# Row norms of half the tiles from a natural-layout load, split query halves kept apart, and new times in the order planner of a two-layer attention trunk

## The chip, the cores and the metric

One core of one Trainium2 chip runs the whole program. The metric is device time in microseconds of one execution; each time given as a result is the median of several executions.

## The reference

A trunk of two layers works on x of 1024 rows by 1024 columns, float32. Each layer adds to x the product of an output matrix with a gated attention result: `x <- x + W_out(mixer(RMSNorm(x)) * silu(gate))`, where one input projection gives queries, keys, values and the gate.

- RMSNorm divides each row of x by the root of its mean square, so it needs one sum of squares for each of the 1024 rows.
- Layer A: 16 query heads of 64 and 2 key heads; each query sees itself and the 127 keys before it, with a learned sink in the softmax.
- Layer B: three groups of 16 query heads and 4 key heads, with (window, dilation) = (128, 1), (512, 4), (2048, 16). The three results are merged for each position by their softmax denominators.
- Queries and keys are normalised for each head, and their first 16 of 64 dimensions are rotated by position.

## The kernel before

**Tiling.** The 1024 rows are 8 row tiles of 128 (`t` or `u`). Columns of the model are 8 blocks of 128 (`k`). Every float32 product is made from two parts: a value is split into a high part in a reduced format (ScalarE, a copy) and a low part, the rest (VectorE or GpSimd, a subtraction), and TensorE makes three products, high by high, high by low, low by high (`split`, line 438; `mm3`, line 500). For each of four sets of heads `n`, `load_w` (452) loads and splits the weights (`raw` to `wt`), and `proj_tile` (505) makes 24 matmuls into `psz` for a row tile, which ScalarE copies to `z`, in layer A with the row's factor `ra`. `z` goes to DRAM (`za`, `zb`) and comes back as `zi` in the order of rows that its group of heads needs (`fetch`, 716).

**Attention of one tile.** `prep` (548) has GpSimd square and rotate, VectorE sum the squares, GpSimd raise to a power (`r`), and TensorE transpose queries and keys into `pq`. ScalarE and VectorE then write the split queries `qs`. Its two halves `two` are the two heads of a pair: ScalarE writes the high part of a half into the upper 64 partitions, VectorE reads that and writes the low part into the lower 64 (lines 571 to 577). `attend` (594) makes the scores `pss`, VectorE adds the mask and takes the minimum (`pe`, with sums of the tile into `nm` or `st`), ScalarE takes the exponential, TensorE transposes it (`ptt`), ScalarE and VectorE split it (`pp`), and TensorE multiplies by the values (`po`). `merge` (642) scales the results: the factors `cr` go to DRAM (`cd`) and come back spread over partitions as `cb`, and VectorE multiplies each result by its `cb`.

**The first row norms.** In the first set of layer A (lines 819 to 846), x arrives transposed by the host (`xt`, partitions are columns). For each row tile it is loaded (`load_xt`, 394) and split into `hT`; then GpSimd squares the whole tile into `sqx`, VectorE sums over `k` into `sr` (rows of the tile along the free side), TensorE transposes `sr` into `pr` in PSUM, VectorE sums that into `ss` (tile `nss`), and `rstd` (470) has GpSimd turn it into `ra`, which scales `z`. `pr` uses a ring of one PSUM buffer that other transposes share (`NB["pM"]` is 1). `sqx` uses a ring of two buffers with the tag `p`, of which the scores `pe` are later users. Later norms (`norm_scale`, 477) take x in natural layout and let ScalarE square and sum in one instruction.

**The order of work.** No loop order is kept. Every call is recorded with its tile regions (`Plan.add`, 172), which are compared element by element for overlaps. `Plan.forward` (209) then plays the program with a priced duration for each instruction (`_price`, 299): each engine takes the ready instruction with the best priority. `backward` (251) makes new priorities from the end, and `issue` (283) tries this for some rounds and keeps the order with the shortest played time. That order is written out for each of the engines, and each engine runs its list strictly in order; all DMAs stand in the one list of SP. A price has two parts, the time until the engine is free and the time until the result is there. A DMA is priced with the issue time `ISSUE`, a fixed time and its bytes at 300 GB/s. All engines' instructions are recorded by a helper, so that the profile puts them on one line (352).

Of the kernel before, what the change touches and what calls it, by code (L numbers as in the profile page):

```python
# [12 lines left out]
F32 = mybir.dt.float32  # L13
F32R = mybir.dt.float32r
# [4 lines left out]
P = 128  # L19
# [27 lines left out]
SECB = 0  # L47
KL = 4
SA = 2
TRIP = 1900  # L50
ROUNDS = 8
SB = 4
YA = 4
# [44 lines left out]
class Plan:  # L98
# [9 lines left out]
           ("POOL", "PE"): 100, ("POOL", "ACT"): 32, ("POOL", "DVE"): 33, ("POOL", "POOL"): 83, ("POOL", "SP"): 100}  # L108
    LOAD = 94
    DRAIN = 25  # L110
    ISSUE = 475

    def __init__(self, tc):
        self.tc, self.nc = tc, tc.nc
# [94 lines left out]
    def forward(self, prio, users):  # L209
        ops, n = self.ops, len(self.ops)  # L210
        left = [len(o[2]) for o in ops]
        start, ready_at = [0.0] * n, [0.0] * n
        free = {e: 0.0 for e in self.ENGINES}
        done = {e: 0.0 for e in self.ENGINES}
        moved = {e: False for e in self.ENGINES}
        future = {e: [] for e in self.ENGINES}
        ready = {e: [] for e in self.ENGINES}
        dma, loaded, order = 0.0, None, []
        for i in range(n):
            if not left[i]:  # L220
                heapq.heappush(future[ops[i][0]], (0.0, i))
        while len(order) < n:
            s, e = min((free[e] if ready[e] else max(free[e], future[e][0][0]), k, e)
                       for k, e in enumerate(self.ENGINES) if ready[e] or future[e])[::2]
            while future[e] and future[e][0][0] <= s:
                i = heapq.heappop(future[e])[1]
                heapq.heappush(ready[e], (prio[i], i))
            i = heapq.heappop(ready[e])[1]
            _, _, _, occ, _, func, dur, _, moves = ops[i]
            wait = 0.0  # L230
            if e == "SP":
                free[e] = s + self.ISSUE
                wait = max(0.0, dma - s - 1100)
                dma = max(dma, s + 1100) + occ
            else:
                if func not in (None, loaded):
                    loaded = func
                    s += 1283
                if moves or moved[e]:
                    s = max(s, done[e] + self.DRAIN)  # L240
                free[e], done[e], moved[e] = s + occ, s + dur, moves
            start[i] = s
            order.append(i)
            for j, t in users[i]:
                ready_at[j] = max(ready_at[j], s + t + wait)
                left[j] -= 1
                if not left[j]:
                    heapq.heappush(future[ops[j][0]], (ready_at[j], j))
        return order, start, max(s + ops[i][6] for i, s in enumerate(start))
# [49 lines left out]
def _price(eng, name, out, ins, kw):  # L299

    n = out.free_size()
    if eng == "SP":
        t = out.size() * 4 / 300.0
        return t, t + 1100 + TRIP
    if eng == "PE":
        t = max(108, (P if name == "transpose" else n) / 2.4 + 13)
        return t, t + 165
    steps = [abs(st) for st, k in out.ap[1:] if k > 1]
    held = any(a.free_size() == 1 for a in ins[1:]) and n > 1
    accum = kw.get("accum_out") is not None  # L310
    if eng == "ACT":
        t = 70 + 0.84 * n + (70 if held else 0) + (0 if ins[0].space == bass.MemoryType.PSUM else 65)
        return (t + 93, t + 73) if accum else (t, t + 90)
    if eng == "DVE":
        if name == "tensor_reduce":
            last = ins[0].ap[-1][0]
            t = 75 + (1.04 if last == 1 else 1.78) * ins[0].free_size()
        elif name == "reciprocal":
            t = 100 + 8 * n
        elif name == "tensor_scalar":  # L320
            t = 130 + 0.53 * n
        else:
            wide = 2.1 if steps and min(steps) >= 4 and n >= 2 * P else 1.04
            t = 70 + wide * n
            t += 80 if name in ("tensor_tensor_reduce", "scalar_tensor_tensor") else 0
        return t, t + 75
    if kw.get("op") is OP.pow:
        t = 270 + 172 * n
    elif n <= 8:
        t = 300  # L330
    else:
        t = 1.95 * n if n > 512 else (50 if 200 < n < 400 else 160) + 2.1 * n
    return t, t + 55
# [23 lines left out]
def trunk(ctx, tc, x, norm_a, w_in_a, q_gain_a, k_gain_a, sinks_a, w_out_a,  # L357
# [190 lines left out]
    def prep(kind, order, tpos, z, nh, kv, slot):  # L548
        w = nh * HD
        sq = nc.tile(sp, [P, 320], F32, tag="sq", bufs=1, name="sq")  # L550
        nc.gpsimd.tensor_tensor(sq[:, :w], z[:, :w], z[:, :w], op=OP.mult)
        ss = nc.tile(sp, [P, 5], F32, tag="ss", bufs=2, name="ss")
        nc.vector.tensor_reduce(ss[:, :nh], sq[:, :w].rearrange("p (h d) -> p h d", d=HD), axis=AX, op=OP.add)
        r = nc.tile(sp, [P, 5], F32, tag="r", bufs=3, name="r")
        rstd(r[:, :nh], ss[:, :nh], 1.0, HD * EPS)
        zr = z[:, :w].rearrange("p (h d) -> p h d", d=HD)[:, :, :ROT]
        t0 = nc.tile(sp, [P, 5, ROT], F32, tag="t0", bufs=1, name="t0")[:, :nh]
        t1 = nc.tile(sp, [P, 5, ROT], F32, tag="t1", bufs=1, name="t1")[:, :nh]
        nc.gpsimd.tensor_tensor(t0, zr, rg[:, kind, :nh], op=OP.mult)
        c_, s_ = cs[:, order, tpos, 0], cs[:, order, tpos, 1]  # L560
        nc.gpsimd.tensor_tensor(t1, t0, c_[:, None, :].to_broadcast([P, nh, ROT]), op=OP.mult)
        hf = ROT // 2
        nc.gpsimd.tensor_tensor(zr[:, :, :hf], t0[:, :, hf:],
                                s_[:, None, :hf].to_broadcast([P, nh, hf]), op=OP.mult)
        nc.gpsimd.tensor_tensor(zr[:, :, hf:], t0[:, :, :hf],
                                s_[:, None, hf:].to_broadcast([P, nh, hf]), op=OP.mult)
        nc.gpsimd.tensor_tensor(zr, zr, t1, op=OP.add)
        pm = nc.tile(pM, [P, 4, P], F32, tag="m", bufs=NB["pM"], name="pq")
        for pr in range(2):
            nc.tensor.transpose(pm[:, pr], z[:, pr * P:(pr + 1) * P], ident)  # L570
        qs = nc.tile(sp, [P, 2, 2, P], F32R, tag="qs", bufs=2, name="qs")
        gq = gc[:, 0, kind:kind + 1]
        for two in range(2):
            rows = slice(two * HD, two * HD + HD)
            nc.scalar.activation(qs[:HD, :, two], pm[rows, 0:2], AF.Copy, scale=gq[rows])
            nc.vector.scalar_tensor_tensor(qs[HD:, :, two], pm[rows, 0:2], gq[rows], f(qs[:HD, :, two]),
                                           op0=OP.mult, op1=OP.subtract)
        if kv is not None:
            kd, vt = kv
            kh, kl = kd[:, 0], kd[:, 1]  # L580
            kk = nc.tile(sp, [P, 2, HD], F32, tag="kk", bufs=2, name="kk")
            nc.gpsimd.tensor_scalar(kk, z[:, None, 4 * HD:5 * HD].to_broadcast([P, 2, HD]), r[:, 4:5], -8.0,
                                    op0=OP.mult, op1=OP.mult)
            nc.tensor.transpose(pm[:, 2], kk.rearrange("p a b -> p (a b)"), ident)
            gk = gc[:, 1, kind:kind + 1]
            nc.scalar.activation(kh[:, slot], pm[:, 2], AF.Copy, scale=gk)
            nc.vector.scalar_tensor_tensor(kl[:, slot], pm[:, 2], gk, f(kh[:, slot]),
                                           op0=OP.mult, op1=OP.subtract)
            zv = z[:, 5 * HD:6 * HD]
            nc.scalar.activation(vt[:, slot, :HD], zv, AF.Copy)  # L590
            nc.gpsimd.tensor_tensor(vt[:, slot, HD:], zv, f(vt[:, slot, :HD]), op=OP.subtract)
        return qs, r
# [220 lines left out]
    for n in range(4):  # L813
# [5 lines left out]
        if n == 0:  # L819
            zd = tc.dram_tile([T, width], F32, name="za0")  # L820
            for t in range(NT):
# [2 lines left out]
                for k in range(0, NK, 4):  # L824
                    split(*(a[:, k:k + 4, t % 2 * P:(t % 2 + 1) * P] for a in hT[t // 2]), xr[:, k:k + 4])
                nc.bias = 0
                sq = nc.tile(sp, [P, NK, P], F32, tag="p", bufs=2, name="sqx")
                if t < SQ:
                    nc.scalar.activation(sq, xr, AF.Square)
                else:  # L830
                    nc.gpsimd.tensor_tensor(sq, xr, xr, op=OP.mult)
                sr = nc.tile(sp, [P, P], F32, tag="zi", bufs=3, name="sr")
                nc.vector.tensor_reduce(sr, sq.rearrange("p k t -> p t k"), axis=AX, op=OP.add)
                pr = nc.tile(pM, [P, 4, P], F32, tag="m", bufs=NB["pM"], name="pr")
                nc.tensor.transpose(pr[:, 0], sr, ident)
                ss = nc.tile(sp, [P, 1], F32, tag="nss", bufs=2, name="nss")
                nc.vector.tensor_reduce(ss, pr[:, 0], axis=AX, op=OP.add)
                rstd(ra[:, t:t + 1], ss, 1.0 / D, EPS)
                if t == LC:
                    late_constants()  # L840
# [222 lines left out]
```

## Time and profile before

| | us |
|---|---|
| median of 3 runs | 1289.6 |
| lowest, highest | 1288.63, 1290.04 |
| the profiled execution | 1286.87 |
| its span, first to last instruction | 1285.0 |
| mean granted TensorE clock | 0.999 |
| ScalarE, VectorE, GpSimd busy | 880.5, 1028.3, 708.3 |
| moved by DMAs | 149.74 MB, 117 GB/s over the span |

The profile is of one execution. PE is TensorE's matmuls, PEld its weight loads, which overlap them, DVE is VectorE, ACT ScalarE, POOL GpSimd, SP the queue that issues the DMAs. Idle time of an engine is put down to what ended it. A wait of an engine that is not the bottleneck costs nothing by itself.

### The profile page before, as it was taken

The page shows a single profiled execution, that of the slowest core. Times are in us where ns is not written, and L with a number is a line of the kernel's source. Part 1 is how long each engine was busy: PE and PEld are TensorE (multiplying, and loading weights), DVE is VectorE, ACT ScalarE, POOL GpSimd, SP SyncE. Part 2 cuts the span into 40 slices and gives each one's busy share as a digit, 9 for nine tenths or more (in the row PEclk, how much of TensorE's full clock was granted, in tenths as well). Part 3 has the DMA queues.
Part 4 walks back from the last instruction along what each step waited for, and adds up shares of the span by engine and source line. Part 5 has one row for each costly group of instructions (what it writes and reads, how often), then busy time and mean ns, then how long its engine had stood idle before and what let it go on. Part 6 is the DMA issues. An engine that isn't in the chain of part 4 may idle for free. (4 is left out here: it accounts for less than half of the span.)

```text
span 1285.0 us, 25754 instructions
## 1 busy us (share of the span) xinstructions
PE 1244.5 (97%) x7851; PEld 1136.3 (88%) x7851; DVE 1028.3 (80%) x2968; ACT 880.5 (69%) x2377; POOL 708.3 (55%) x1388
## 2 busy tenths in 40 slices
PE   7999999999999999999999999999999999999998
PEld 6999899998688999989888999988999988998776
DVE  8668888777955428878888878889888989779896
ACT  5367686877733437877767887767887766987661
POOL 5655455455500038556567655477656567786632
PEclk9999999999999999999999999999999999999999
DMA  6423223245444233223233323244233244454525
GB/s 226 141 76 103 84 80 117 81 146 178 123 129 140 99 104 99 81 71 111 93 125 122 91 73 111 88 139 135 79 95 91 94 130 128 140 174 129 173 80 181
DMA packets 142666, 149.74 MB, mean 117 GB/s; under 512 B 33576, under 2 KB 129344, under 8 KB 142528
## 3 DMA queue, kind: packets, MB, share of 16 engines
q1 hardware_dynamic: 142528, 148.09, 36.7%
q8 instruction: 63, 1.03, 0.3%
q14 instruction: 75, 0.61, 0.2%
HBM read 105.57 MB, written 42.47 MB: 115 GB/s over the span
## 5 line engine op out<-in xcount | busy, mean ns | idle before, releaser
L352 PE MATMUL psz<-wt,hT 128*128 128x384 f32 (+1 forms) x3072 | 632.9, 343 | 5.7 <-DVE wt L352 2.8
L352 PEld LDWEIGHTS psz<-wt,hT 128*128 128x128 f32 x3072 | 510.8, 190 | 16.2 <-DVE wt L352 3.6
L352 PE MATMUL psg<-hT,wt 128*128 128x256 f32 x1536 | 220.3, 291 | 0.3 <-DVE gT L352 0.3
L352 PEld LDWEIGHTS psg<-hT,wt 128*128 128x128 f32 x1536 | 200.3, 191 | 2.3 <-PE psg L352 0.5
L352 ACT ACTIVATE pe<-pe,st 128x128 f32<-128x128 f32 (+1 forms) x384 | 169.1, 442 | 36.2 <-DVE st L352 33.7
L352 PE MATMUL ptt<-ident,pe 128*128 128x128 f32 x800 | 170.8, 275 | 2.8 <-ACT pe L352 2.6
L352 DVE SCALAR_TENSOR_TENSOR qs<-pq,gt,qs 64x256 fp32r<-64x256 f32 x256 | 123.9, 484 | 44.8 <-ACT qs L352 38.5
L352 DVE TENSOR_TENSOR pp<-ptt,pp 128x512 fp32r<-128x512 f32 x200 | 131.5, 684 | 32.2 <-ACT pp L352 30.6
L352 POOL TENSOR_TENSOR r<-r,ex 128x5 f32<-128x5 f32 (+1 forms) x128 | 150.6, 1176 | 5.6
L352 ACT ACTIVATE qs<-pq,gt 64x256 fp32r<-64x256 f32 x256 | 120.1, 469 | 42.9 <-PE pq L352 36.2
L352 DVE SCALAR_TENSOR_TENSOR wt<-raw,gt,wt 128x384 fp32r<-128x384 f32 (+1 forms) x188 | 114.5, 639 | 28.5 <-ACT wt L352 26.6
L352 ACT ACTIVATE pp<-ptt 128x512 fp32r<-128x512 f32 x200 | 111.9, 595 | 35.9 <-PE ptt L352 35.1
L352 ACT ACTIVATE oh<-po 64x512 f32<-64x512 f32 x128 | 76.0, 594 | 82.2 <-PE po L352 78.5
L352 DVE CUSTOM_DVE_ANT_0 pe<-pss,con,r 128x256 f32<-128x256 f32 x288 | 123.5, 477 | 8.9 <-PE pss L352 8.5
L352 PEld LDWEIGHTS ptt<-ident,pe 128*128 128x128 f32 x800 | 105.7, 140 | 21.8 <-ACT pe L352 9.8
L352 ACT ACTIVATE wt<-raw,gt 128x384 fp32r<-128x384 f32 (+1 forms) x188 | 98.9, 564 | 19.6 <-DMA raw<-in_w_in_b_dram 6.9
L352 PE MATMUL po<-pp,vring 128*128 128x512 f32 x280 | 106.9, 416 | 3.8 <-ACT pp L352 1.5
L352 POOL TENSOR_SCALAR r<-ss 128x5 f32<-128x5 f32 (+1 forms) x128 | 30.3, 237 | 144.7 <-DVE st L352 55.5
L352 PE MATMUL psw<-hT,wy 128*128 128x512 f32 x384 | 107.8, 408 | 2.0 <-ACT wy L352 1.2
L352 POOL TENSOR_TENSOR sq<-zi 128x320 f32<-128x320 f32 (+1 forms) x128 | 93.8, 733 | 25.3 <-DMA zi<-za 9.8
L352 PE MATMUL pss<-kring,qs 128*128 128x256 f32 x560 | 99.3, 286 | 2.5 <-DVE kring L352 2.3
L352 POOL TENSOR_TENSOR t<-zi,rg 128x80 f32<-128x80 f32 (+1 forms) x128 | 48.4, 378 | 93.3 <-DMA zi<-zb 60.2
(142 smaller groups left out, 2175.3 us busy)
## 6 DMA issues: line engine op xcount, KB each, us to landing
raw<-in_w_in_b_dram SPq DMA_DIRECT2D x96, 192.0 KB
zb<-z SPq DMA_DIRECT2D x96, 192.0 KB
cb<-cd SPq DMA_DIRECT2D x128, 128.0 KB
zi<-zb SPq DMA_DIRECT2D x64, 192.0 KB
raw<-in_w_in_a_dram SPq DMA_DIRECT2D x48, 128.0 KB
yraw<-yd SPq DMA_DIRECT2D x24, 256.0 KB
zi<-zb SPq DMA_DIRECT2D x64, 96.0 KB
xt<-in_xt_dram SPq DMA_DIRECT2D x16, 256.0 KB
```

What stands on the lines that cost most here:

```text
L352: self.plan.add(self.name, method, lambda: fn(*args, **kw), outs, ins, price, func)
```

## The change

Three things change. In odd row tiles of the first set, x is also loaded in natural layout (`xn`, 512 KB), and ScalarE squares it and sums along the free side in one instruction; squares on GpSimd, the sum over `k`, the transpose `pr` and its sum stay for the even tiles. The tile `qs` keeps its two halves in separate stretches of memory, and is used through a view with the old order of indices. The planner's prices change: a DMA's fixed time from 1100 + 1900 to 500 + 1150 ns, the issue from 475 to 520, and several formulas for instructions.

```diff
-TRIP = 1900
+LEAD = 500
+TRIP = 1150
...
-    ISSUE = 475
+    ISSUE = 520
...
-                wait = max(0.0, dma - s - 1100)
-                dma = max(dma, s + 1100) + occ
+                wait = max(0.0, dma - s - LEAD)
+                dma = max(dma, s + LEAD) + occ
...
-        return t, t + 1100 + TRIP
+        return t, t + LEAD + TRIP
...
+    psum = bool(ins) and ins[0].space == bass.MemoryType.PSUM
     if eng == "ACT":
-        t = 70 + 0.84 * n + (70 if held else 0) + (0 if ins[0].space == bass.MemoryType.PSUM else 65)
-        return (t + 93, t + 73) if accum else (t, t + 90)
+        if accum:
+            return 342 + 0.625 * n, 284 + 0.84 * n
+        t = 70 + 0.84 * n + (70 if held else 0) + (0 if psum else min(75, 0.4 * n) + 25 * held)
+        return t, t + 90
     if eng == "DVE":
         if name == "tensor_reduce":
-            last = ins[0].ap[-1][0]
-            t = 75 + (1.04 if last == 1 else 1.78) * ins[0].free_size()
-        elif name == "reciprocal":
+            t = 80 + (1.04 if ins[0].ap[-1][0] == 1 else 1.78) * ins[0].free_size()
+            return t, t + 65
+        if name == "reciprocal":
             t = 100 + 8 * n
         elif name == "tensor_scalar":
             t = 130 + 0.53 * n
+        elif n <= 16:
+            return 105, 215
         else:
-            wide = 2.1 if steps and min(steps) >= 4 and n >= 2 * P else 1.04
-            t = 70 + wide * n
-            t += 80 if name in ("tensor_tensor_reduce", "scalar_tensor_tensor") else 0
-        return t, t + 75
+            t = 70 + 1.04 * n
+            if name in ("tensor_tensor_reduce", "scalar_tensor_tensor"):
+                t += 60 if psum else 105
+            elif steps and min(steps) >= 4:
+                return (70 + 1.82 * n, 145 + 1.82 * n) if n >= 2 * P else (70 + 1.18 * n, 220 + 1.18 * n)
+        return t, t + 78
     if kw.get("op") is OP.pow:
         t = 270 + 172 * n
-    elif n <= 8:
-        t = 300
+    elif name == "tensor_scalar":
+        return 300 + 1.25 * n, 235 + 1.35 * n
...
-        qs = nc.tile(sp, [P, 2, 2, P], F32R, tag="qs", bufs=2, name="qs")
+        qs = nc.tile(sp, [P, 2, 2, P], F32R, tag="qs", bufs=2, name="qs").rearrange("p two pr q -> p pr two q")
...
-                sq = nc.tile(sp, [P, NK, P], F32, tag="p", bufs=2, name="sqx")
...
+                if t % 2:
+                    xn = nc.tile(sp, [P, D], F32, tag="p", bufs=2, name="xn")
+                    nc.sync.dma_start(xn, x[t * P:(t + 1) * P])
+                    ss = nc.tile(sp, [P, 1], F32, tag="nss", bufs=2, name="nss")
+                    nc.scalar.activation(xn, xn, AF.Square, accum_out=ss)
                 else:
-                    nc.gpsimd.tensor_tensor(sq, xr, xr, op=OP.mult)
...
+                    sq = nc.tile(sp, [P, NK, P], F32, tag="p", bufs=2, name="sqx")
...
                 rstd(ra[:, t:t + 1], ss, 1.0 / D, EPS)
```

## Rows read from the trace of the kernel before

**Rows 1.** The page's first part: busy time, share of the span, instructions.

```profile
PE 1244.5 (97%) x7851; PEld 1136.3 (88%) x7851; DVE 1028.3 (80%) x2968; ACT 880.5 (69%) x2377; POOL 708.3 (55%) x1388
```

**Rows 2.** Busy time by stretch: length, engines, granted clock, DMA share, GB/s.

```profile
0.00:40.00 40.00, 28.80 (x138) 26.98 (x139) 33.92 (x38) 18.89 (x33) 23.21 (x24) 1.00 0.62 208
40.00:1240.00 1200.00, 1176.73 (x7535) 1079.22 (x7534) 961.77 (x2850) 850.16 (x2314) 673.88 (x1357) 1.00 0.36 112
1240.00:1285.00 45.00, 38.93 (x182) 30.11 (x180) 32.64 (x82) 11.44 (x30) 11.18 (x9) 1.00 0.45 156
...
6.60:13.30 6.70, 3.45 (x8) 2.15 (x8) 6.70 (x8) 5.41 (x12) 1.96 (x1) 1.00 0.81 295
13.30:19.20 5.90, 5.89 (x18) 5.89 (x19) 5.90 (x9) 0.33 (x1) 3.39 (x3) 1.00 0.78 266
19.20:31.70 12.50, 12.50 (x74) 12.40 (x74) 10.81 (x11) 7.60 (x14) 8.44 (x8) 1.00 0.57 190
```

**Rows 3.** Waits, whole run: who for whom, us in total, times, longest.

```profile
DVE qs L352 <- ACT qs L352: 38.5, 55, 4.6
...
PEld ptt L352 <- ACT pe L352: 9.8, 32, 1.0
...
PEld pss L352 <- DVE qs L352: 2.3, 4, 0.8
...
DVE og L352 <- DMA cb<-cd: 2.2, 3, 1.5
```

**Rows 4.** Groups of instructions by shape: count, busy us, mean ns, idle before.

```profile
L352 DVE SCALAR_TENSOR_TENSOR wt<-raw,gt,wt 128x384 fp32r<-128x384 f32 x108 | 70.4, 680 | 20.4 <-ACT wt L352 19.3
...
L352 ACT ACTIVATION_READ_ACCUMULATOR pe<-pe,st 128x1 f32 x384 | 71.9, 187 | 0.0
...
L352 ACT ACTIVATE wt<-raw,gt 128x384 fp32r<-128x384 f32 x108 | 62.2, 611 | 16.8 <-DMA raw<-in_w_in_b_dram 6.9 <-PE psw L352 6.3 <-PE psg L352 1.9
...
L352 DVE TENSOR_TENSOR og<-po,oh 64x256 f32<-64x256 f32 x64 | 39.6, 618 | 1.6
...
L352 POOL TENSOR_SCALAR r<-ss 128x5 f32<-128x5 f32 x112 | 27.2, 243 | 126.9 <-DVE st L352 55.5 <-DVE ss L352 45.5 <-DVE nm L352 21.7
...
L352 POOL TENSOR_TENSOR sqx<-xt 128x1024 f32<-128x1024 f32 x8 | 15.9, 1986 | 9.8 <-DMA xt<-in_xt_dram 9.5
L352 DVE TENSOR_REDUCE sr<-sqx 128x128 f32<-128x1024 f32 x8 | 15.8, 1980 | 0.0
...
L352 ACT ACTIVATE hn<-part 128x1024 f32<-128x1024 f32 x6 | 6.4, 1062 | 12.7 <-DVE part L352 12.7
```

**Rows 5.** Instructions in order of time, startup: start us, length us, what, idle before.

```profile
7.03 1.14 DVE L352 SCALAR_TENSOR_TENSOR wt<-raw,gt,wt 128x384 fp32r<-128x384 f32 x2
...
10.88 1.96 POOL L352 TENSOR_TENSOR sqx<-xt 128x1024 f32<-128x1024 f32 x1 [4.32 <-DMA xt<-in_xt_dram]
11.01 2.77 DVE L352 SCALAR_TENSOR_TENSOR wt<-raw,gt,wt 128x384 fp32r<-128x384 f32 x2
...
13.31 8.88 PE L352 MATMUL psz<-wt,hT 128*128 128x384 f32 x34 [2.42 <-DVE wt L352]
...
33.73 0.33 PE L352 MATMUL pr<-ident,sr 128*128 128x128 f32 x1 [1.58 <-DVE nss L352]
```

**Rows 6.** Instructions in order of time, the two writers of `qs`, three tiles.

```profile
61.20 0.95 ACT L352 ACTIVATE qs<-pq,gt 64x256 fp32r<-64x256 f32 x2 [4.99 <-PE pq L352]
62.18 0.98 DVE L352 SCALAR_TENSOR_TENSOR qs<-pq,gt,qs 64x256 fp32r<-64x256 f32 x2 [4.63 <-ACT qs L352]
...
646.92 0.47 ACT L352 ACTIVATE qs<-pq,gt 64x256 fp32r<-64x256 f32 x1 [0.38 <-DVE qs L352]
...
1135.12 0.98 DVE L352 SCALAR_TENSOR_TENSOR qs<-pq,gt,qs 64x256 fp32r<-64x256 f32 x2 [0.35 <-ACT qs L352]
```

**Rows 7.** Instructions in order of time, one load of `zi` and its first reader.

```profile
125.52 0.33 SPq L352 DMA_DIRECT2D zi<-za  x1
...
127.58 0.32 POOL L352 TENSOR_TENSOR t<-zi,rg 128x64 f32<-128x64 f32 x1 [5.71 <-DMA zi<-za]
```

**Rows 8.** The chain that ended last: start us, us, what.

```profile
1266.98 4.09 DMA cb<-cd
```

More of the change, by code (lines that the diff above doesn't have):

```diff
@@ L826, in trunk @@
                 nc.bias = 0
-                sq = nc.tile(sp, [P, NK, P], F32, tag="p", bufs=2, name="sqx")
-                if t < SQ:
-                    nc.scalar.activation(sq, xr, AF.Square)
-                else:
-                    nc.gpsimd.tensor_tensor(sq, xr, xr, op=OP.mult)
[L832 to L837, printed above, removed]
+                if t % 2:
[3 more added lines that the diff above has]
+                    nc.scalar.activation(xn, xn, AF.Square, accum_out=ss)
+                else:
+                    sq = nc.tile(sp, [P, NK, P], F32, tag="p", bufs=2, name="sqx")
+                    if t < SQ:
+                        nc.scalar.activation(sq, xr, AF.Square)
+                    else:
+                        nc.gpsimd.tensor_tensor(sq, xr, xr, op=OP.mult)
+                    sr = nc.tile(sp, [P, P], F32, tag="zi", bufs=3, name="sr")
+                    nc.vector.tensor_reduce(sr, sq.rearrange("p k t -> p t k"), axis=AX, op=OP.add)
+                    pr = nc.tile(pM, [P, 4, P], F32, tag="m", bufs=NB["pM"], name="pr")
+                    nc.tensor.transpose(pr[:, 0], sr, ident)
+                    ss = nc.tile(sp, [P, 1], F32, tag="nss", bufs=2, name="nss")
+                    nc.vector.tensor_reduce(ss, pr[:, 0], axis=AX, op=OP.add)
                 rstd(ra[:, t:t + 1], ss, 1.0 / D, EPS)
```

## The prediction

> **What bounds the kernel now.** I read the page's busy times first, then three stretches side by side, then the waits of the weight loads, then the startup in order of time, the costs of the operations touched, the chain of waits, and last the two instructions that write the split queries. TensorE is busy 97% of the span [rows 1], so what the other engines do is worth only the idle time that it takes from TensorE. That is 1285.0 - 1244.5 = 40.5 us, and the three stretches say where it lies: 40 - 28.8 = 11.2 us in the first 40, 1200 - 1176.7 = 23.3 us in the next 1200, 45 - 38.9 = 6.1 us in the last 45 [rows 2]. No wait stands out in the long middle: the weight loads' largest is 9.8 us over 32 occasions [rows 3]. So the kernel is bound by TensorE's own work, plus a startup, plus many waits of under 1 us that come from the written order of the engines meeting real durations.
>
> **Part 1: odd row tiles, 4 of 8.** Removed for each odd tile: GpSimd's squaring (1.99 us), VectorE's sum over k (1.98 us), the transpose `pr` and a small sum of it on VectorE. Added: a 512 KB load on SP's queue and a ScalarE squaring with its sum; the nearest row, the same operation in `norm_scale`, takes 1.06 us and the read of a sum after it 0.19 us [rows 4]. Over four tiles: GpSimd -8.0, VectorE -7.9, ScalarE +5.0 us, and four transposes that I count as nothing. ScalarE is busy 18.9 of the first 40 us [rows 2], and that idle time hides the 5.0 us; without it each square would delay one `z` by 1.25 us.
>
> What is on the path: TensorE's first long run, 34 matmuls, starts at 13.31 after a wait of 2.42 us for VectorE's `wt` [rows 5]. That `wt` is a pair of low halves that took 2.77 us from 11.01, where the pair at 7.03 took 1.14. GpSimd squares tile 1 from 10.88 to 12.84, over just that time [rows 5]. With tile 1 on ScalarE the pair should take 1.14, so TensorE's run starts 2.77 - 1.14 = 1.6 us earlier. Tile 0 is even and keeps its sum on VectorE ahead of these, so this edit moves the run no further up. Later TensorE stops 1.58 us at 33.73 before a `pr`, until the `nss` of the tile before has read the one PSUM buffer of that ring [rows 5]; with half of the `pr` gone I let this go, and see nothing late next: the matmuls behind it had their data. Sum -3.2 us.
>
> Against this stand 2.1 MB more in a stretch where the transfers are dense: 295 and 266 GB/s at a share of 0.81 and 0.78 between 6.6 and 19.2 us, then 190 GB/s [rows 2]. One load within the dense part is 0.52 MB at 0.28 MB per us, 1.9 us ahead of weights or of the next tile; those of tiles 3, 5 and 7 come later, where the share is 0.57. Each `xn` also takes a place in a ring of two that the even tiles' squares use, so SP's queue may stand before the load until an older tile is read, with the next `xt` and the weights queued behind it. Bounds: 0 (it lands in free time) and +7.6 us (four times 1.9). I take +1.0, nearer to the lower end, since only tile 1's load is surely in the dense part and TensorE has a run of 34 matmuls queued then. Part 1: -3.2 + 1.0 = -2.2 us.
>
> **Part 2: the halves of `qs`.** The planner counts exact overlaps, so for it ScalarE's second write and VectorE's first one have nothing to do with each other. The trace says otherwise. At 61.20 ScalarE writes both halves in 0.95 us, and VectorE, idle for 4.63 us, starts only at 62.18, after the second. At 1135.12 the same after 0.35 us idle. Where VectorE's first comes before ScalarE's second, ScalarE waits for it, 0.38 us before 646.92 [rows 6]. In the old layout each half's two pieces lie around a piece of the other, so that the stretches from first to last byte cross; I take this for the cause. With the halves apart VectorE's first can go about 0.47 us earlier. I count 44 of 128 query tiles where VectorE starts over 0.15 us after both its own last instruction and ScalarE's first half were done, the first and the last those at 62.18 and 1135.12, together 17.9 us; VectorE's whole wait for `qs` is 38.5 us in 55 occasions [rows 3, 6]. Upper bound for TensorE 17.9 us; lower 0, since VectorE is busy 80% [rows 1] and such delays mostly end in its own idle time. The nearest row is the weight loads' wait for `qs` itself, 2.3 us in 4 occasions [rows 3]. I take -2.5: that row and a little for what VectorE does behind `qs`.
>
> **Part 3: the planner's times.** They move no work, but all five engines' orders are made anew, SP's with them. Old price, new price and measured mean of the whole instruction, in ns: GpSimd's `r<-ss` 355, 242, 243; VectorE's `og` of 64x256 683, 611, 618; its `wt` of 384 columns 624, 652, 680; ScalarE's `wt` 617, 652, 611 (worse) [rows 4]. The large change is the transfer: 1100 + 1900 becomes 500 + 1150 ns, beside the size at 300 GB/s. The 128 KB `zi` issued at 125.52 is used at 127.58, 2.06 us after; old price 3.44, new 2.09 [rows 7]. In a dense stretch the new price is too short: a 128 KB `cb` of the last merge takes 4.09 us [rows 8].
>
> What is a better model worth? Of the 23.3 idle us in the middle most are small misfits of order. Bounds: all of them and half of the last 6.1, some -26, and by symmetry +26 if the new order fits as much worse. Most priced durations come nearer to the measured ones, and so does the most frequent load, so I expect a gain, but a greedy order shifts by chance too. I take -3.0, an eighth of the middle's idle time.
>
> [...] For the 128 KB load the row gives 2.06 us [rows 7]. [...]
>
> **Sum.** -2.2 - 2.5 - 3.0 = -7.7 us. The profiled execution took 1286.87 us, its span 1285.0 and 1.87 around it; after, 1279.2. The median of the runs shown, 1289.6, is 2.7 above that execution, so the forecast is 1289.6 - 7.7 = 1281.9.
>
> **Rivals.**
> (a) A larger gain: the parts add up at their deep ends, startup -3.2, `qs` -6 (a third of its bound), order -10, which gives 1270.4. For it: VectorE loses 7.9 us of work and up to 17.9 of waiting, and is the nearest to TensorE in busy time [rows 1]. Against: the waits for it are spread thin.
> (b) Slower: the short price of a transfer turns VectorE's queue into the wait. The place is `merge`: 64 multiplications by a `cb` stand in VectorE's order, now planned 1.35 us sooner after their load. VectorE waits for a `cb` only 2.2 us in 3 occasions before [rows 3], since the old price was long enough. If a third of the 64 wait 1.0 us (half of what the 4.09 us load exceeds 2.09 by), that is 21 us of VectorE, with the next tile's `pe`, `qs` and `pp` behind it; at half reaching TensorE +10.5. With startup and `qs` as above: 1289.6 - 4.7 + 10.5 = 1295.4. It decides once VectorE's waits for `cb` pass some 10 us. Against: the transfers' share in the middle is 0.36 [rows 2], so most loads run beside little else.
> (c) No change: the stops removed come back elsewhere, the 2.1 MB cost what the startup gives, and the new order is as good as the old: 1289.
> (d) Not what it says: if VectorE's late start at `qs` has another cause than the layout, that part gives 0: 1284.4, within the forecast's own range.
>
> **Chances.** Forecast with (d), 1276 to 1287: 0.44. (a): 0.20. (c), 1287 to 1292.2: 0.14. (b): 0.22. A difference under 0.2% (2.6 us) can't be told from none, so faster means under 1287.0: 0.44 + 0.20 = 0.64; same 0.14; slower 0.22. The range from 1267 to 1297 leaves out the far ends of (a) and (b), about 0.08 each; the forecast's own is 1276 to 1287.
>
> **What would show it.** Startup: TensorE's long run from about 11.7 rather than 13.3, four `pr` in place of eight, four ScalarE squares of `xn`, and no pair of `wt` of over 1.5 us beside tile 1. `qs`: VectorE's first starts within 0.1 us of the end of ScalarE's first wherever it was idle, and its wait for `qs` falls from 38.5 to about 20 us. Order: TensorE's idle time between 40 and 1240 near 18 in place of 23.3. The prediction is wrong if VectorE's waits for `cb` or GpSimd's for `zi` grow by tens of us, if the first 46 us get longer, or if new stops of some 2 us appear in the middle.

## The result: 0.6% slower, and the profile after

After the change the kernel takes 1297.1 us (median of 4 runs, 1294.19 to 1298.18), beside 1289.1 us for the kernel before in the same runs (1288.46 to 1290.04): ratio 1.0058, 95% interval 1.0043 to 1.0073. The forecast was 1281.9, a gain, so it lies on the wrong side of no change; rival (b), the transfer price that makes VectorE stand at `cb`, had given 1295.4. The rows below come from one execution of 1294.19 us, span 1292.3.

The first line of the page, after. It answers to [rows 1].

```profile
PE 1242.8 (96%) x7847; PEld 1134.0 (88%) x7847; DVE 1020.5 (79%) x2960; ACT 885.0 (68%) x2383; POOL 699.2 (54%) x1384
```

Every engine has less work or about as much (ScalarE 4.5 us more, as planned), four matmuls are gone, and the span is 7.3 us longer. So TensorE's idle time must have grown. Busy time by stretch, after (the columns of [rows 2]), says where:

```profile
0.00:40.00 40.00, 32.09 (x163) 30.34 (x164) 29.46 (x41) 22.12 (x40) 15.70 (x24) 1.00 0.79 264
40.00:1240.00 1200.00, 1165.42 (x7481) 1069.05 (x7480) 955.53 (x2834) 851.20 (x2313) 673.18 (x1353) 1.00 0.36 112
1240.00:1292.30 52.30, 45.24 (x206) 34.58 (x206) 35.53 (x87) 11.65 (x30) 10.31 (x8) 0.99 0.40 142
```

Length less TensorE's busy time is its idle time: 11.2 to 7.9 us in the first 40 us, 23.3 to 34.6 in the middle, 6.1 to 7.1 at the end. The startup gained 3.3 us, near the forecast; the middle lost 11.3 us, where I had forecast a gain of 5.

The waits after, in the form of [rows 3]:

```profile
DVE qs L360 <- ACT qs L360: 24.6, 45, 3.4
PEld ptt L360 <- ACT pe L360: 19.5, 39, 2.4
PEld po L360 <- DVE pp L360: 12.0, 26, 2.2
DVE og L360 <- DMA cb<-cd: 10.8, 11, 2.9
DVE oa L360 <- DMA cb<-cd: 10.7, 7, 5.2
...
DVE o L360 <- DMA cb<-cd: 3.9, 5, 2.0
```

VectorE's waits for `cb` were 2.2 us in 3 occasions; now three lines name them, 10.8 + 10.7 + 3.9 = 25.4 us in 23. The weight loads' waits for `pe` doubled, 9.8 to 19.5 us, and those of `po` for VectorE's `pp` rose from 8.0 to 12.0 us.

One such place in order of time, after: a load of `cb`, the multiplication by it, and what VectorE does behind it, until TensorE moves again.

```profile
873.86 1.26 SPq L360 DMA_DIRECT2D cb<-cd  x2
...
876.41 0.34 DVE L360 SCALAR_TENSOR_TENSOR kring<-pq,gt,kring 128x128 fp32r<-128x128 f32 x1
...
879.65 0.69 DVE L360 TENSOR_TENSOR og<-og,cb 128x512 f32<-128x512 f32 x1 [2.90 <-DMA cb<-cd]
...
880.65 0.75 DVE L360 TENSOR_TENSOR pe<-pss,con 128x256 f32<-128x256 f32 x2
...
881.71 0.40 ACT L360 ACTIVATE pe<-pe,st 128x128 f32<-128x128 f32 x1 [2.63 <-DVE st L360]
...
882.25 0.47 PE L360 MATMUL ptt<-ident,pe 128*128 128x128 f32 x1 [2.10 <-ACT pe L360]
```

The two loads are issued from 873.86 to 875.12. VectorE is done with `kring` at 876.75, its next instruction in the written order is the multiplication, and it stands until 879.65, 5.8 us after the first issue and 4.5 us after the end of the second. The scores `pss` had been ready meanwhile; their mask and row minimum (`pe`, `st`) start only after it, ScalarE's exponentials wait 2.63 us for them, and TensorE stops 2.10 us. Price of the load in the plan: 2.09 us.

### The profile page after: what moved, and what is told of

Its sections match the earlier page's. It is cut to its first block, busy times and chain, and to the rows that moved or that the text cites. A ratio compares the mean times of both kernels' runs of the same rounds, so it can differ in the third digit from the quotient of the medians.

```text
span 1292.3 us, 25704 instructions
## 1 busy us (share of the span) xinstructions
PE 1242.8 (96%) x7847; PEld 1134.0 (88%) x7847; DVE 1020.5 (79%) x2960; ACT 885.0 (68%) x2383; POOL 699.2 (54%) x1384
## 4 chain that ended last, share of the span: by engine, by line
PE 51%; DVE 13%; DMA 8%; POOL 2%; ACT 2%; issue 2%; SPq 1%; DVEq 0%; POOLq 0%; ACTq 0%
PE psz L360 22%; PE psw L360 8%; PE psg L360 7%; PE po L360 4%; DMA cb<-cd 4%; PE pss L360 4%; PE ptt L360 4%; DVE pe L360 2%; PE pq L360 2%; DMA zi<-zb 2%; DVE pp L360 1%; SPq L360 1%; DVE og L360 1%; DVE qs L360 1%; DMA cd<-cr 1%
## 5 line engine op out<-in xcount | busy, mean ns | idle before, releaser
L360 PE MATMUL ptt<-ident,pe 128*128 128x128 f32 x800 | 174.8, 276 | 9.3 <-ACT pe L360 9.0
L360 DVE TENSOR_TENSOR pp<-ptt,pp 128x512 fp32r<-128x512 f32 x200 | 131.6, 683 | 28.8 <-ACT pp L360 27.3
L360 DVE SCALAR_TENSOR_TENSOR qs<-pq,gt,qs 64x256 fp32r<-64x256 f32 x256 | 123.8, 484 | 30.9 <-ACT qs L360 24.6
L360 PEld LDWEIGHTS ptt<-ident,pe 128*128 128x128 f32 x800 | 105.9, 140 | 31.4 <-ACT pe L360 19.5
L360 DVE SCALAR_TENSOR_TENSOR wt<-raw,gt,wt 128x384 fp32r<-128x384 f32 (+1 forms) x188 | 108.5, 608 | 21.7 <-ACT wt L360 20.5
L360 POOL TENSOR_TENSOR t<-zi,rg 128x80 f32<-128x80 f32 (+1 forms) x128 | 48.8, 381 | 108.8 <-DMA zi<-zb 79.9
L360 POOL TENSOR_TENSOR sq<-zi 128x320 f32<-128x320 f32 (+1 forms) x128 | 94.7, 740 | 23.2 <-DMA zi<-za 11.1
```

The lines of the kernel that those rows point to most:

```text
L360: self.plan.add(self.name, method, lambda: fn(*args, **kw), outs, ins, price, func)
```

## The experiments

Each ratio is against the kernel before, run on the same chip in the same session (1290.4 to 1290.8 us there, 1289.1 beside after), with its 95% interval. There were three such sessions, e1 to e4, e5 to e8 and e9 to e12, each on another chip; a step from one session to another is taken between the ratios. The fourth column is VectorE's wait for `cb` (us, times), the last TensorE's idle time in 40 to 1240 us; both are read from the profiled execution as above.

| kernel | median us (runs) | ratio | wait for `cb` | idle |
|---|---|---|---|---|
| before | 1289.1 (4) | 1 | 2.2, 3 | 23.3 |
| after | 1297.1 (4) | 1.0058 (1.0043 to 1.0073) | 25.4, 23 | 34.6 |
| e1_old_prices | 1282.9 (6) | 0.9936 (0.9921 to 0.9950) | 2.9, 6 | 22.2 |
| e2_new_prices_only | 1295.8 (7) | 1.0034 (1.0023 to 1.0046) | 18.7, 24 | 29.1 |
| e3_old_dma_price | 1274.6 (4) | 0.9871 (0.9855 to 0.9888) | 1.7, 1 | 20.2 |
| e4_new_dma_price_only | 1302.2 (6) | 1.0083 (1.0066 to 1.0100) | 16.8, 21 | 35.4 |
| e5_cb_long | 1277.2 (6) | 0.9904 (0.9879 to 0.9929) | 4.1, 5 | 23.5 |
| e6_cb_short | 1290.0 (12) | 1.0013 (0.9993 to 1.0032) | 32.5, 35 | 31.9 |
| e7_no_cb_wait | 1283.7 (7) | 0.9952 (0.9933 to 0.9971) | 0.7, 1 | 27.3 |
| e8_mid_price | 1291.0 (12) | 1.0007 (0.9988 to 1.0026) | 7.3, 10 | 29.2 |
| e9_old_qs_layout | 1272.7 (4) | 0.9863 (0.9847 to 0.9878) | 3.3, 6 | 19.1 |
| e10_no_pq_read | 1275.0 (5) | 0.9873 (0.9851 to 0.9895) | 4.4, 7 | 19.2 |
| e11_nudge | 1276.8 (5) | 0.9896 (0.9880 to 0.9911) | 3.6, 4 | 23.2 |
| e12_cb_longer | 1274.0 (4) | 0.9871 (0.9856 to 0.9886) | 0.6, 1 | 17.5 |

**Which part costs: four kernels.** e1 is the kernel after with all the old prices back; e2 the kernel before with all the new ones; e3 the kernel after with the old transfer price alone; e4 the kernel before with the new transfer price alone. The edit of e3 (that of e4 is the reverse, in the kernel before):

```diff
-LEAD = 500
-TRIP = 1150
+LEAD = 1100
+TRIP = 1900
...
-    ISSUE = 520
+    ISSUE = 475
```

> The change with all of the planner's prices as they were (transfer 1100 + 1900, issue 475, old formulas); natural load and separate halves stay. Theory P (the new prices cost the time): the startup's gain of some 3 us stays and the middle comes back, 1283 to 1288. Theory S (the natural load or the new qs layout costs it): 1294 to 1298. Theory C (any new order is a draw by chance): anywhere from 1282 to 1298, with no relation to which price is old.

> The kernel before with all new prices, without the natural load and with the old qs layout. Theory P: slower than before by what the change lost and the startup's gain on top, 1297 to 1301. Theory S: 1286 to 1290. Theory C: anywhere from 1285 to 1300.

> The change with the old transfer price and issue time alone (1100 + 1900, 475), new formulas for the engines. If the short transfer price is the cause (rival b): as with all old prices, 1283 to 1288, and VectorE's waits for cb fall from about 23 us in all to under 6. If the engines' new formulas are the cause: 1293 to 1298, waits for cb under 6 all the same.

> The kernel before with the new transfer price and issue time alone (500 + 1150, 520). If the short transfer price is the cause: 1296 to 1300, VectorE's waits for cb over 15 us. If the engines' new formulas are the cause: 1287 to 1291, whatever the waits for cb are.

Read as steps from one kernel to the next: the new transfer price costs 0.83% on the old code and formulas (before to e4) and 1.87% on the new ones (e3 to after, 24 us of 1290). The new engine formulas gain 0.49% beside the short price (e4 to e2) and 0.65% beside the long one (e1 to e3). Parts 1 and 2 gain 0.64% at the old prices (before to e1) and lose 0.24% at the new ones (e2 to after). So the transfer price alone makes the change a loss, and e3 beats both kernels by more than 1%. Each of these steps is one pair of orders, and below it is seen that a new order alone can move the time by some 0.3%. The expectations missed in places: e3 was put at 1283 to 1288, as if the engine formulas were worth nothing, and came out 9 us lower; e2 came out 1.2 us under its range, e4 2.2 us above. The middle stretch of e3:

```profile
40.00:1240.00 1200.00, 1179.83 (x7588) 1086.32 (x7587) 967.20 (x2883) 860.17 (x2341) 684.25 (x1358) 1.00 0.37 114
```

TensorE does 1179.83 us of work there, against 1165.42 after.

**Is it `cb`, among all transfers?** e5 is the kernel after with only `cb` and the store `cd` ahead of it priced as before; e6 is e3 with only these two priced short. (The remarks behind `#`, here and below, are not in the code.)

```diff
-        return t, t + LEAD + TRIP
+        merge = out.name.startswith(("cb", "cd"))
+        return t, t + LEAD + TRIP + (1350 if merge else 0)     # e5; in e6: - (1350 if merge else 0)
```

> The change, with the transfers of the merge alone (cd and cb) priced 1350 ns longer, as long as before; all other transfers short. If the place is the merge (VectorE stands at cb): most of the loss goes, 1276 to 1286, VectorE's waits for cb under 8 us in place of 25. If all short transfers share the loss (zi and raw as much): 1286 to 1294, with the waits for cb gone and GpSimd's for zi still near 128 us. Theory C (each order a draw): no relation.

> The mirror of it: the change with the old transfer price for all but cd and cb, which are short. If the place is the merge: 1288 to 1298, waits for cb over 15 us. If the loss is shared: 1278 to 1286. Theory C: no relation.

e5 regains 1.54% of the 1.87%, e6 loses 1.42%: the two are mirror images. No run separates `cb` from `cd`. In e6 the waits for `cb` are back, more of them than after, and no other transfer is priced short:

```profile
DVE o L361 <- DMA cb<-cd: 12.8, 12, 2.2
DVE og L361 <- DMA cb<-cd: 11.8, 13, 2.1
...
DVE oa L361 <- DMA cb<-cd: 7.1, 9, 1.4
```

In e5 GpSimd goes on waiting for its `zi`, whose price is still short:

```profile
POOL t L361 <- DMA zi<-zb: 69.6, 27, 34.5
...
POOL sq L361 <- DMA zi<-zb: 12.7, 10, 3.7
```

That is 82.3 us; after it is 79.9 + 7.9 = 87.8, before 60.2 + 0.6 = 60.8. GpSimd is busy 54% and has room: its longer waits, the second sign that the prediction named as its refutation, cost nothing that these runs can tell.

The total of the waits for `cb` does not rank the kernels: e4 has 16.8 us of them and is the slowest, e6 has 32.5 and is 0.7% faster than that. The order that comes with a price counts as well as the standing.

**The wait or the order?** e7 has the order of the kernel after, instruction for instruction, but VectorE multiplies by a table that lies in memory from the start in place of `cb` (the loads are still made).

```diff
...
-            nc.vector.tensor_tensor(os[i], os[i], cb, op=OP.mult)
+            nc.vector.tensor_tensor(os[i], os[i], cb, op=OP.mult,
+                                    instead=con[:, :4 * P].rearrange("p (a q) -> p a q", a=2))
```

> The change in its own order, instruction for instruction, but VectorE's multiplications by cb read a resident constant in place of cb (the result is not the reference's); all transfers are still issued. If VectorE's standing at cb is the loss: 1278 to 1288. If it is mostly hidden: 1291 to 1297.

```profile
40.00:1240.00 1200.00, 1172.71 (x7516) 1076.64 (x7514) 962.79 (x2855) 855.27 (x2326) 677.42 (x1356) 1.00 0.37 112
```

VectorE's wait for `cb` falls by 24.7 us, TensorE's idle time over the whole span (span less busy time) from 49.5 to 40.2, and the time by 8.7 us between the profiled executions, by 1.06% (13.7 us) between the ratios. So the wait itself is shown to cost 9 to 14 us, a third to somewhat over a half of its length. It is not all: e7 still stands 0.81% above e3. That part lies in the order that the short price gives and not in standing at `cb`. Of the 10.5 us between the two spans, 40.2 - 36.3 = 3.9 are TensorE's idle time and 6.6 its busy time (1243.5 us in e7, 1236.9 in e3, with the same matmuls), whose ends are modelled; which places of the order make it up stays open.

**How long must the price be?** e8 puts the whole round trip at 500 + 1800 ns for all transfers, between new and old; e12 is e3 with `cb` and `cd` 1000 ns longer still.

```diff
-TRIP = 1150
+TRIP = 1800          # e8, LEAD stays 500
...
+        return t, t + LEAD + TRIP + (1000 if merge else 0)     # e12, on e3
```

> The change with 500 + 1800 ns for a transfer, between the two prices. If a short price costs by late loads, the time lies between: 1278 to 1290, waits for cb 5 to 15 us. Theory C: anywhere from 1272 to 1300.

> e3_old_dma_price with cd and cb priced 1000 ns longer still (4000 and the bytes). If late loads at cb are already gone at the old price (waits for cb 1.7 us): no gain, ratio 0.984 to 0.991. If a longer price helps further by itself: 0.983 or less.

e12 equals e3: a price of `cb` and `cd` longer than needed costs nothing here. e8 lies between after and e3 (1 us above its expected range), with 7.3 us of waits for `cb`; that is too little to explain 1.36% above e3 by standing at `cb`, and agrees with what e7 left over.

**What does the layout of `qs` do?** e9 is e3 with the old layout; order and waits are the same. In e10, also on e3 and in its order, VectorE's low halves read a constant in place of `pq` in PSUM, so that ScalarE alone reads `pq`.

```diff
...
-        qs = nc.tile(sp, [P, 2, 2, P], F32R, tag="qs", bufs=2, name="qs").rearrange("p two pr q -> p pr two q")
+        qs = nc.tile(sp, [P, 2, 2, P], F32R, tag="qs", bufs=2, name="qs")          # e9
...
-                                           op0=OP.mult, op1=OP.subtract)
+                                           op0=OP.mult, op1=OP.subtract,           # e10
+                                           instead=con[rows, :2 * P].rearrange("p (a q) -> p a q", a=2))
```

> The change with the old transfer price (as e3_old_dma_price) and the old layout of qs: the same order and the same waits, instruction for instruction. If the layout is worth something: 2 us or more slower than e3_old_dma_price, ratio 0.989 or more. If it does nothing: ratio 0.986 to 0.988, and VectorE's waits for qs as there.

> e3_old_dma_price in its own order, but VectorE's low halves of qs read a resident constant in place of the PSUM tile pq that ScalarE reads too (the result is not the reference's). Theory PSUM (two readers of one PSUM tile are put one after the other): VectorE's first starts within 0.1 us of the end of ScalarE's first where it is idle, its waits for qs fall by 10 to 20 us, the time by 1 to 5 us, ratio 0.983 to 0.986. Theory layout or delayed signal: the late starts stay, ratio 0.987.

e9 and e3 are the same within their intervals: the layout does nothing that can be told. After the change VectorE's first still starts when ScalarE's second is done:

```profile
50.02 0.95 ACT L360 ACTIVATE qs<-pq,gt 64x256 fp32r<-64x256 f32 x2 [1.01 <-PE pq L360]
...
51.00 0.98 DVE L360 SCALAR_TENSOR_TENSOR qs<-pq,gt,qs 64x256 fp32r<-64x256 f32 x2 [1.48 <-ACT qs L360]
```

In e10 it starts after ScalarE's first, half way through the pair:

```profile
53.98 0.97 ACT L363 ACTIVATE qs<-pq,gt 64x256 fp32r<-64x256 f32 x2 [0.39 <-PE pq L363]
...
54.48 0.99 DVE L363 SCALAR_TENSOR_TENSOR qs<-con,gt,qs 64x256 fp32r<-64x256 f32 x2 [0.29 <-ACT qs L363]
```

By the count of the prediction, 44 tiles before and 42 after start late, 44 in e3 and 42 in e9; in e10 none. Its wait line, where e3 has 28.2 us in 44 occasions:

```profile
DVE qs L363 <- ACT qs L363: 11.5, 13, 4.1
```

So the late start comes from both engines reading the one tile `pq`: the two readers follow one another. Whether a semaphore that the program sets or the memory itself asks for that, no run separates. The two read different partitions, VectorE's first 0 to 63 and ScalarE's second 64 to 127; yet of the 368 reads of `pq` by each of the two engines no two overlap in time, in the trace before or in that after. No gain in time is seen, where e10 had been put at 0.983 to 0.986: 16.7 us less of waiting leave 0.9871 at 0.9873. That is not a clean price of the late start, for in e10 the low halves themselves take longer and GpSimd is busy 28.0 us more (last section).

**How much is chance?** e11 is e3 with TRIP at 1910 in place of 1900, a change of 10 ns that can mean nothing of itself.

```diff
-TRIP = 1900
+TRIP = 1910
```

> e3_old_dma_price with 1910 in place of 1900 ns: a price that is the same for all purposes, but gives another order. It measures the draw of the order: within 4 us of e3_old_dma_price (ratio 0.984 to 0.990) if orders of like prices are alike; further off if each order is a draw, and then differences of that size between other kernels here say nothing about a price.

It moved the time by 0.25%; the two intervals just overlap. One such draw is no distribution, but differences of some 0.3% between two orders made anew (e5 to e3, or Parts 1 and 2 beside the new prices) prove nothing. e7, e9 and e10 are free of this, since they keep the order.

## Why the prediction was wrong, point by point

**Part 1 (odd tiles) came as worked out; how much of it lasts is open.** The startup after, in order of time, beside [rows 5]:

```profile
6.78 0.48 SPq L360 DMA_DIRECT2D xn<-in_x_dram  x1
...
10.96 1.14 DVE L360 SCALAR_TENSOR_TENSOR wt<-raw,gt,wt 128x384 fp32r<-128x384 f32 x2
...
11.62 11.91 PE L360 MATMUL psz<-wt,hT 128*128 128x384 f32 x58 [0.76 <-DVE wt L360]
...
12.60 2.92 POOL L360 TENSOR_TENSOR sqx<-xt 128x1024 f32<-128x1024 f32 x1 [6.07 <-DMA xt<-in_xt_dram]
...
13.79 1.06 ACT L360 ACTIVATE xn<-xn 128x1024 f32<-128x1024 f32 x1
13.88 3.38 DVE L360 TENSOR_TENSOR hT<-xt,hT 128x512 fp32r<-128x512 f32 x3
...
48.05 0.27 PE L360 MATMUL pr<-ident,ra 128*8 128x128 f32 x1 [1.48 <-POOL ra L360]
```

The pair of `wt` takes 1.14 us in place of 2.77, the long run starts at 11.62 (forecast 11.7), the square takes the 1.06 us of its row, and TensorE has 3.3 us more done at 40 us (forecast 3.2 before the cost of the loads). Not all of that is Part 1: e2, the new prices without it, has 30.39 us done at 40 us, so the rest gives 1.7 beside the new prices (e2 to after) and 2.8 beside the old (28.80 to 31.58 in e1), around the forecast of 2.2. By 60 us TensorE is busy 49.80 us, 48.80 before. These are single executions: e3 and e9, which have one order, read 30.28 and 31.00 at 40 us and 48.85 and 49.91 at 60, so a difference of 1.0 there proves nothing. One place where time is given back is the transpose of all the `ra` at 48.05, which waits 1.48 us for GpSimd and before waited for nothing. The square of the next even tile (12.60) now lies beside VectorE's splits of `hT`, but all 16 of these take 15.2 us before and after.

**Part 2 (halves of `qs`): the observation held, the cause did not.** VectorE did start after ScalarE's second, as read from [rows 6]; that the crossing bytes of the layout were why was only argued, and e9 and e10 refute it. Rival (d) was right, and the term of -2.5 is 0. VectorE's whole wait for `qs` did fall from 38.5 to 24.6 us, near the 20 that the prediction named as its sign, but by luck: with the new layout and the old prices (e1) it is 36.3 us in 51 occasions, so the fall comes with the new order.

**Part 3 (prices): the step that failed.** I took -3.0 as one sum for two things, because most priced durations come nearer to the measured ones "and so does the most frequent load". Taken apart, the engine formulas gain more than that (0.65%, 8.4 us, e1 to e3), and the transfer price loses 24 us (e3 to after). For `cb` the new price does not come nearer. In the trace of the kernel before, its 128 loads of 128 KB land 2.8 to 5.5 us after their issue, median 3.1 (from the issue to the last signal of the landing), against an old price of 3.44 and a new one of 2.09: not one lands within the new price. Plain loads of the same size do fit it: those of `raw` (48 in layer A, 32 in layer B) have medians of 2.13 and 2.15 us there. Why those of `cb` take longer stays open; each spreads one row of DRAM over 64 partitions, and no run varies that. I had both rows for it: 2.06 us from issue to use for one `zi` [rows 7] and 4.09 us for a `cb` [rows 8]. I took the first as the rule, since the transfers' share in the middle is 0.36 [rows 2], and the second as the exception of a dense stretch (share 0.83 over its 4.09 us). But what the price decides is how long VectorE stands at `cb`, so the row to go by was that of `cb`. In the kernel after, they land 2.8 to 5.4 us after their issue, median 3.1 again; e8's price for them, 2.74 us, is still under the shortest.

**Rival (b) was right in the place and near in the size; its total agrees in part by luck.** It had a third of 64 multiplications wait 1.0 us, 21 us, half of it reaching TensorE: +10.5. Measured: 23 of 64, 1.1 us each, 25.4 us, and 9 to 14 us of time. But its 1295.4 had nothing for the rest of the 24 us, which lies in the order, and nothing for the 8.4 us that the engine formulas gain; it took 4.7 for the startup and `qs`, of which the 2.5 for `qs` came to nothing. These errors partly cancel. What argued against it ("most loads run beside little else") was true and beside the point: a load of `cb` takes its 3 us at a share of 0.36 too. A chance of 0.22 was too low, for I had one row just under the new price (2.06 against 2.09 us) and one at twice it.

**The expected gain of the middle** (5 us) thus turned into 11.3 us more of TensorE's idle time. Of the 19.1 us between the profiled spans of e3 and after, 49.5 - 36.3 = 13.2 us are idle time; the other 5.9 lie in TensorE's busy time, whose ends are modelled, and can't be told apart here. Not tried: bringing the loads of `cb` forward, and a price of its own for every kind of transfer.

## What to carry to other kernels

A planner's price of a transfer is a bet on the engine that waits for it, and the two sides are unlike: 1 us longer than before cost nothing here (e12), 1.35 us shorter cost over 1% (e5, e6), in part because VectorE, in its written order, stood at one load with all that was queued behind it (2.90 us up to 879.65, after). Set the price of each kind of load from the landings of that kind, those first that a busy engine waits for: here one size had a median of 2.1 us in one kind and 3.1 in another. And change it apart from the engines' prices. Before explaining a start that is late by one instruction, ask which operand the engines share, the one written or the one read.

## What the runs showed of the hardware that I had not expected

TensorE's clock fell around one long stop. The stretches around the stop at 882 us, after (columns of [rows 2]):

```profile
880.00:884.00 4.00, 1.90 (x7) 1.58 (x7) 3.92 (x17) 2.24 (x9) 3.33 (x5) 0.76 0.35 98
884.00:888.00 4.00, 4.00 (x27) 3.79 (x26) 3.62 (x9) 2.98 (x8) 2.97 (x6) 0.81 0.43 128
```

The granted clock averages 0.76 in the first and 0.81 in the next; cut finer, it is 0.50 from 882.25 to 885.50 and 1.00 from 886 on. TensorE had stood from 880.15 to 882.25. Two matmuls of `psz` ahead of the stop and two behind it:

```profile
874.89 0.60 PE L360 MATMUL psz<-wt,hT 128*128 128x384 f32 x2
...
882.38 0.99 PE L360 MATMUL psz<-wt,hT 128*128 128x384 f32 x2
```

So this stop of 2.10 us cost something beyond its own length: the pair behind it takes 0.39 us more. The kernel before has such a place too, around a stop of 1.97 us that ends at 326.94 (0.80 and 0.77 in 324 to 332 us), so this isn't what the change lost. It does not follow every stop of that length: after one of 2.00 us that ends at 210.78, after, the clock stays at 1.00.

GpSimd was slower where VectorE read SBUF in place of PSUM. In e10 VectorE's 256 low halves read SBUF in place of PSUM, with the same instructions in the same order as e3. The page's first line of e3:

```profile
PE 1236.9 (97%) x7847; PEld 1135.2 (89%) x7847; DVE 1016.5 (80%) x2960; ACT 883.9 (69%) x2383; POOL 707.0 (56%) x1384
```

And of e10:

```profile
PE 1234.6 (97%) x7847; PEld 1135.7 (89%) x7847; DVE 1026.2 (81%) x2960; ACT 883.8 (70%) x2383; POOL 735.0 (58%) x1384
```

GpSimd's 1384 instructions take 28.0 us more and VectorE's 9.7, with ScalarE unmoved; e9, in the same order, has 707.0 us of GpSimd as e3 has. VectorE's part lies in the changed instructions themselves, 527 ns each in place of 484; GpSimd's are the same as before. So a change of what VectorE reads went here with 4% more busy time of GpSimd; what joins the two no run separates. In the startup it was VectorE that ran slower beside GpSimd: its pair of `wt` took 2.77 us beside a square [rows 5], and 1.14 after, where GpSimd stood idle.
